# Feed-forward activations turned by transposing transfers of 16 bit halves instead of by TensorE

## The chip, the cores and the metric

The kernel runs on one core of a Trainium2 chip. The metric is the device time of one execution in microseconds (us), the median of several runs. Engines are named as the profile names them: PE is TensorE (matrix products and transposes) and PEld its weight loader, DVE is VectorE, ACT is ScalarE, POOL is GpSimd and SP the engine that issues most transfers. A "q" behind an engine's name (ACTq, SPq) stands for its issuing of transfers.

## The reference

One decoder layer for 256 tokens and a model width of 2048. The part that matters here is the feed-forward at its end, in float32:

```
h = x + concatenate([gla_out, nsa_out]) @ w_out
m = rms_norm(h, ffn_norm_g)
return h + (silu(m @ w_gate) * (m @ w_up)) @ w_down        # w_gate, w_up: 2048 x 5632, w_down: 5632 x 2048
```

The attention parts ahead of it are not touched by the change.

## The kernel before

The feed-forward runs over 11 blocks of 512 hidden columns (NFB = 11, FB = 512). For each block f, `gate_up(f)` forms the gate and up products in PE's banks, eight pairs of row tiles at a time, most of them with seven products instead of eight (the banks q = 1, 5, 6, 7 hold sums that are combined on DVE afterwards). Its last steps give two tiles `g` of 128 tokens by 512 hidden values, kept in `hidden[f]`. `down(f)` multiplies them with `w_down`, and needs them turned: hidden values on the partitions. The program runs gate_up(0), gate_up(1), down(0), gate_up(2), down(1) and so on; the last block has a `down_last` of its own.

All products use float32 operands split into two rounded parts, hi and lo: ACT copies a tile into hi with rounding, DVE subtracts to get lo (`in_parts`, lines 654 to 657). The same is done with every weight tile that arrives: `fraw` is the raw tile, `ftwo` its parts, and `fsum` and some tiles `g` are sums of weight rows.

The turn is `turn_act(fb, qs)`: for each of the two tiles, four 128 x 128 transposes on PE (line 213, with the identity `ident`) into a bank, then hi and lo of that bank into `acts[fb]`, which `down` reads. It is a generator in the queue `urgent`; while the main generator `gate_up(fb + 1)` emits products, `drive` calls `side` now and then, which lets the first waiting side task take its next step. A number that a task yields puts it to sleep for that many calls. For block 0 the turn is queued near the end of gate_up(1), for blocks 1 to 9 at the start of the next gate_up, and for block 10 ahead of down(9). Within `gate_up`, a pair that is not among the "sevens" drains `urgent` first, because its products and the turns share bank 8.

Within `down`, each of four stretches n of 512 output columns is started from `h_sb[n]`, which ACT copies into two banks (`seed`, line 1281), and its results are copied back out of the banks by ACT (line 1293). Those banks are then used by the next `gate_up`.

What a side task emits is not executed at once: a scheduler lays the instructions of each engine out in one fixed order before the program runs, and each engine works through its own in that order. An instruction that has to wait holds up everything behind it on its engine, including the issue of transfers. Tiles named `f` come from a pool of six (`g2` in this stage), tiles `g` from one of 24.

Of the kernel before, what the change touches and what calls it, by code (L numbers as in the profile page):

```python
# [7 lines left out]

F32 = mybir.dt.float32
F32R = mybir.dt.float32r  # L10
BF16 = mybir.dt.bfloat16
AF = mybir.ActivationFunctionType
ALU = mybir.AluOpType
# [2 lines left out]
P = 128  # L16
S = 256
# [20 lines left out]
def kernel(  # L38
# [4 lines left out]
    nc = tc.nc  # L43
    act, mm = nc.scalar.activation, nc.tensor.matmul
# [22 lines left out]
    g4, g2, g1, small = slot(gp, "g4", 24, LINE), slot(s2p, "g2", 13), slot(s1p, "g1", 7), slot(s1p, "sm", 12)  # L67
# [8 lines left out]

    def f32(t):
        return t.bitcast(F32)


    urgent, later, background = [], [], []
# [41 lines left out]

    def weight(tag, nk, w, bufs, dt=F32R):
        n_tiles[0] += 1
# [227 lines left out]
    def first_chunk(q):  # L353
        nonlocal first_rest
        hi, lo = g4([4, S], F32R), g4([4, S], F32R)
        n_h.append(hi)
# [285 lines left out]
    def gla_turn(h, y):  # L642
        yield 26
        if h % 2 == 0:
            m_h[h // 2], m_l[h // 2] = g4([4, S], F32R), g4([4, S], F32R)
        p = bank()
# [7 lines left out]
    def in_parts(hi, lo, ps, after=None):  # L654
        with behind(after):
            act(hi, ps, AF.Copy)  # L656
        last["d"] = TT(lo, ps, f32(hi), ALU.subtract)  # L657
# [505 lines left out]
    def gate_up(fb):  # L1163
        def product(q, a, w, k):

            if q not in banks:
                banks[q] = bank()
            for x, m in ((a[0], w[k][0]), (a[0], w[k][1]), (a[1], w[k][0])):
                mm(banks[q], x, m, start=todo[q] == total[q], stop=todo[q] == 1)  # L1169
                todo[q] -= 1  # L1170

        def tokens(k, t):
            assert k in turned
            return tuple(x[k // 4][:, k % 4, t * P:(t + 1) * P] for x in (hT_h, hT_l))

        order, sevens = (ORDER0, ORDER1, ORDER)[0 if fb == 0 else 1 if fb < ALL7 else 2], FIRST7.get(fb, PAIRS7)
        last7 = max(sevens, key=order.index)
        todo = dict.fromkeys((1, 5, 6, 7), 3 * len(sevens))
        todo.update(dict.fromkeys((2, 3, 4), 3 * len(sevens) + 6 * (8 - len(sevens))))
        todo[8] = 6 * (8 - len(sevens))  # L1180
        total = dict(todo)
        if fb > 1:
            urgent.append(turn_act(fb - 1, (8, 8)))
        for at, pair in enumerate(order):
            if fb > 1 and pair not in sevens:
                drain(urgent)
            if fb == 0 and at == len(OLD):
                ffn_pools()
            a, b = 2 * pair, 2 * pair + 1
            ready = row_sums.get((fb, pair))  # L1190
            if at < 7:
                fetch_sums(fb, order[at + 1])
            r = load4([(w_gate[0], a, 2, fb * FB), (w_up[0], a, 1 if ready else 2, fb * FB)])
            if ready:
                s1, s2 = fetched.pop((fb, pair))
            if pair in sevens:
                w = parts_of(r[:, 0:3])
                if not ready:
                    s1, s2 = g4([2, 512]), fw["sum"]([2, 512])
                    TT(s1, r[:, 1:3], r[:, 3:4].to_broadcast([P, 2, 512]), ALU.add)  # L1200
                    TT(s2[:, 0], s1[:, 1], r[:, 1], ALU.add)
                    TT(s2[:, 1], s2[:, 0], r[:, 0], ALU.add)  # L1202
                f = [tuple(forms[pair][:, i, j] for i in range(2)) for j in range(4)]
                raw = {1: (tokens(b, 0), 1), 2: (tokens(a, 0), 0), 3: (f[3], 2)}
                of_sums = {5: (f[0], 0), 7: (f[2], 1), 6: (f[1], 2), 4: (tokens(a, 1), 3)}

                for q in (6, 1, 5, 7, 2, 3, 4) if at == 7 else (1, 2, 3, 5, 7, 6, 4):
                    if q in of_sums and len(of_sums) == 4:
                        ws = parts_of2(s1, s2)
                        if ready:  # L1210
                            ws = [ws[k] for k in (1, 0, 3, 2)]
                    if q in raw:
                        x, k = raw[q]
                        product(q, x, w, k)
                    else:
                        x, k = of_sums.pop(q)
                        product(q, x, ws, k)
                    yield 2
            else:
                w = parts_of(r)  # L1220
                for q, t, m in ((2, 0, 0), (3, 0, 1), (4, 1, 0), (8, 1, 1)):
                    for j in range(2):
                        product(q, tokens(a + j, t), w, 2 * m + j)
                        yield 2
            if pair == last7:
                q1, u, q5u, q7u, q57u = (g2([512]) for _ in range(5))
                act(q1, banks[1], AF.Copy)
                TT(u, banks[6], q1, ALU.add)
                TT(q5u, banks[5], u, ALU.subtract)
                TT(q7u, banks[7], u, ALU.add)  # L1230
                TT(q57u, banks[5], q7u, ALU.subtract)
                if fb == 1:
                    urgent.append(turn_act(0, (1, 5)))
                if fb:
                    seed(0, DOWN[min(fb - 1, 1)])
        if fb == 0:
            drain(urgent)
            rms(rf, ssh)
            TT(rf, rf, hback, ALU.mult)
        gs = hidden[fb] = []  # L1240
        for t, (g, gq, u_, uq) in enumerate(((q1, 2, q5u, 3), (q7u, 4, q57u, 8))):
            TT(g, banks[gq], g, ALU.add)
            act(g, g, AF.Silu, scale=rf[:, t:t + 1])
            if total[uq]:
                TT(u_, banks[uq], u_, ALU.add)
            STT(g, u_, rf[:, t:t + 1], g, ALU.mult, ALU.mult)
            gs.append(g)

    hidden, acts = {}, {}

    def turn_act(fb, qs):
        for _ in range(2):
            yield
        gs = hidden.pop(fb)
        hi, lo = acts[fb] = g4([4, S], F32R), g4([4, S], F32R)
        for t in range(NT):
            ts = slice(t * P, (t + 1) * P)
            p = banks[qs[t]]
            for j in range(4):
                transpose(p[:, j * P:(j + 1) * P], gs[t][:, j * P:(j + 1) * P])  # L1260
                if j % 2:
                    yield
            pv = p.rearrange("p (j s) -> p j s", j=4)
            in_parts(hi[:, :, ts], lo[:, :, ts], pv)
        if fb == NFB - 1:
            for pair in range(2):
                yield
                yield
                v, ks = g2([2, S]), slice(2 * pair, 2 * pair + 2)
                TT(v, f32(hi[:, ks]), f32(lo[:, ks]), ALU.add)  # L1270
                pair_forms(8 + pair, v)
# [164 lines left out]
```

## Time and profile before

| | us |
|---|---|
| median of three runs | 1102.14 (1101.81 to 1103.24) |
| the profiled execution, its own time | 1101.13 |
| its span, first to last instruction | 1099.1 |
| PE busy | 1094.3 |
| DVE busy | 996.3 |
| ACT busy | 744.5 |
| POOL busy | 81.1 |

The granted clock of PE is 1.000 throughout. The profile lists groups of instructions by line, engine and operation (busy time, mean duration in ns, idle time before them and who ended it), a table of busy time by stretch, each engine's instructions in order of time with the idle time before each in brackets, and the transfers with the time from issue to landing.

### The profile page before, as it was taken

To read this page: it belongs to the slowest core of one execution; us is meant where nothing else is said; L and a number is where in the kernel's file an instruction comes from. 1 tells how busy PE (TensorE), PEld (TensorE's weight loads), DVE (VectorE), ACT (ScalarE), POOL (GpSimd) and SP (SyncE) were. 2 spreads that over 40 slices of the span, in tenths; PEclk is the share of its full clock that TensorE was granted. 3 is DMA by queue.
4 is the path that set the end of the run, shared out by engine and by line. 5 is a ranking of instruction groups with operands and counts; after the bars stand their busy time and mean duration, and the time that the engine had idled before them with its cause. 6 is when DMAs were issued, how large, how long until landed. Compare 5 with 4: busy or idle time off the path is not lost.

```text
span 1099.1 us, 14686 instructions
## 1 busy us (share of the span) xinstructions
PE 1094.3 (100%) x5294; PEld 900.8 (82%) x5294; DVE 996.3 (91%) x1289; ACT 744.5 (68%) x1014; POOL 81.1 (7%) x150
## 2 busy tenths in 40 slices
PE   9999999999999999999999999999999999999998
PEld 8888888987777887888888888888888888888887
DVE  6578879987799988997999999999999999999998
ACT  7645567555675587667585867768585877768685
POOL 4110001033100100000000000000000000000000
PEclk9999999999999999999999999999999999999999
DMA  7999978468886946785566657576665768677663
GB/s 271 340 338 369 394 259 284 167 243 290 307 280 246 331 159 244 234 317 190 182 230 209 211 197 253 184 248 209 213 230 202 251 214 294 208 259 232 235 231 115
DMA packets 128818, 271.15 MB, mean 247 GB/s; under 512 B 7093, under 2 KB 9177, under 8 KB 128746
## 3 DMA queue, kind: packets, MB, share of 16 engines
q1 hardware_dynamic: 115466, 223.61, 59.2%
q0 software_dynamic: 12672, 46.14, 11.3%
q8 instruction: 41, 0.67, 0.2%
q10 hardware_dynamic: 608, 0.47, 0.1%
q14 instruction: 31, 0.25, 0.1%
HBM read 247.12 MB, written 23.07 MB: 246 GB/s over the span
## 4 chain that ended last, share of the span: by engine, by line
PE 89%; DVE 3%; DMA 3%; issue 2%; ACT 2%; POOL 0%; SPq 0%; DVEq 0%; ACTq 0%; POOLq 0%
PE bank L289 41%; PE bank L1169 39%; PE bank L213 3%; DMA g<-in_w_up_dram 2%; PE bank L1310 2%; DVE lo L145 2%; PE bank L967 1%; PE bank L893 1%; DMA raw<-in_w_out_dram 1%; DVE g L1101 1%; ACT hi L144 1%; PE bank L598 0%; PE bank L800 0%; PE bank L203 0%; ACT g L559 0%
## 5 line engine op out<-in xcount | busy, mean ns | idle before, releaser
L1169 PE MATMUL bank<-ftwo,g 128*128 128x512 f32 x1842 | 430.7, 393 | 0.2 <-ACT ftwo L656 0.2
L1169 PEld LDWEIGHTS bank<-ftwo,g 128*128 128x128 f32 x1842 | 341.2, 188 | 77.0 <-DVE ftwo L657 4.0
L289 PE MATMUL bank<-hi,g 128*128 128x512 f32 (+1 forms) x1088 | 322.7, 377 | 0.0
L657 DVE TENSOR_TENSOR ftwo<-fraw,ftwo 128x1536 fp32r<-128x1536 f32 (+1 forms) x130 | 256.8, 1976 | 7.7 <-ACT ftwo L656 6.6
L656 ACT ACTIVATE ftwo<-fraw 128x1536 fp32r<-128x1536 f32 (+1 forms) x130 | 216.0, 1663 | 28.9 <-DMA fraw<-in_w_up_dram 19.1
L289 PE MATMUL bank<-ftwo,g 128*128 128x512 f32 x960 | 220.7, 390 | 0.0
L289 PEld LDWEIGHTS bank<-hi,g 128*128 128x128 f32 x1088 | 191.9, 189 | 30.3 <-issue 1.0
L289 PEld LDWEIGHTS bank<-ftwo,g 128*128 128x128 f32 x960 | 179.7, 188 | 38.3 <-ACT bank L1281 0.3
L144 ACT ACTIVATE hi<-raw 128x1024 fp32r<-128x1024 f32 (+3 forms) x124 | 130.4, 1058 | 94.7 <-PE bank L289 67.1
L289 PE MATMUL bank<-lo,g 128*128 128x512 f32 (+3 forms) x544 | 193.3, 376 | 0.4 <-DVE lo L145 0.3
L145 DVE TENSOR_TENSOR lo<-raw,hi 128x1024 fp32r<-128x1024 f32 (+3 forms) x124 | 149.8, 1217 | 29.6 <-ACT hi L144 29.3
L656 ACT ACTIVATE ftwo<-g 128x1024 fp32r<-128x1024 f32 x76 | 80.4, 1057 | 73.2 <-DVE g L1200 49.9
L289 PEld LDWEIGHTS bank<-lo,g 128*128 128x128 f32 x544 | 98.2, 189 | 15.2 <-DVE lo L145 1.0
L657 DVE TENSOR_TENSOR ftwo<-g,ftwo 128x1024 fp32r<-128x1024 f32 x76 | 92.8, 1221 | 10.3 <-ACT ftwo L656 10.3
L657 DVE TENSOR_TENSOR ftwo<-fsum,ftwo 128x1024 fp32r<-128x1024 f32 x76 | 92.7, 1220 | 1.0 <-ACT ftwo L656 1.0
L656 ACT ACTIVATE ftwo<-fsum 128x1024 fp32r<-128x1024 f32 x76 | 79.6, 1048 | 5.5 <-DVE fsum L1202 3.9
L1293 ACT COPY g<-bank 128x512 f32<-128x512 f32 x80 | 45.9, 588 | 38.6 <-PE bank L289 36.9
L1200 DVE TENSOR_TENSOR g<-fraw 128x1024 f32<-128x1024 f32 x54 | 65.3, 1220 | 0.3 <-DMA fraw<-in_w_up_dram 0.3
L1281 ACT COPY bank<-g 128x512 f32<-128x512 f32 x80 | 45.3, 594 | 14.7 <-DVE f L1230 8.4
L1158 POOL DMA_DIRECT2D g<-sums x20 | 10.6, 531 | 502.1 <-DVE ftwo L657 473.6
L656 ACT ACTIVATE g<-bank 128x512 fp32r<-128x512 f32 x46 | 26.9, 597 | 29.7 <-PE bank L213 21.2
L213 PE MATMUL bank<-ident,g 128*128 128x128 f32 (+3 forms) x230 | 42.9, 277 | 0.1
(249 smaller groups left out, 913.2 us busy)
## 6 DMA issues: line engine op xcount, KB each, us to landing
fraw<-in_w_gate_dram SPq DMA_DIRECT2D x86, 512.0 KB, 4.0
fraw<-in_w_down_dram SPq DMA_DIRECT2D x42, 1024.0 KB, 5.0
raw<-in_w_in_dram SPq DMA_DIRECT2D x36, 1024.0 KB, 7.8
fraw<-in_w_up_dram SPq DMA_DIRECT2D x66, 512.0 KB, 4.8
sums<-g POOLq DMA_DIRECT2D x40, 512.0 KB, 6.5
raw<-in_w_out_dram SPq DMA_DIRECT2D x16, 1024.0 KB, 7.3
g<-in_w_gate_dram SPq DMA_DIRECT2D x20, 512.0 KB, 7.5
g<-in_w_up_dram SPq DMA_DIRECT2D x20, 512.0 KB, 7.8
```

What stands on the lines that cost most here:

```text
L144: act(h[:, i:i + n], r[:, k + i:k + i + n], AF.Copy)
L145: last["d"] = TT(o[:, i:i + n], r[:, k + i:k + i + n], f32(h[:, i:i + n]), ALU.subtract)
L213: return nc.tensor.transpose(o, i, ident[:n, :n])
L289: last["mm"] = mm(bk[t], a[:, k, t * P:(t + 1) * P], ws[k][m][:, off:off + w], start=(first_ and k == 0 and i == 0), stop=(end and k == 3 ...
L656: act(hi, ps, AF.Copy)
L657: last["d"] = TT(lo, ps, f32(hi), ALU.subtract)
L893: mm(sv, a[:, j], b, start=(i == 0), stop=False, skip_group_check=True)
L1169: mm(banks[q], x, m, start=todo[q] == total[q], stop=todo[q] == 1)
L1200: TT(s1, r[:, 1:3], r[:, 3:4].to_broadcast([P, 2, 512]), ALU.add)
L1281: last["seed", n] = nc.scalar.copy(banks[qs[n][t]], h_sb[n][:, t, :])
L1293: nc.scalar.copy(h_sb[n][:, t, :], bs[t])
L1310: mm(bk, u, m, start=(first and i == 0), stop=(end and i == 2), skip_group_check=onto)
```

## The change

`turn_far` takes the place of `turn_act` for blocks 0 to 9. It treats each float32 value as two 16 bit halves. For each tile, ACT copies the halves apart (all upper, all lower) into a tile `u`, and issues a transposing transfer from `u` back into the tile `g`, in 16 bit elements. Six calls of `side` later, ACT copies the halves together again into `u`, and hi and lo are made from `u`. For block 0 the turn is queued at the start of gate_up(1) instead of its end. Block 10 keeps `turn_act`.

```diff
+    def u16(t):
+        return t.bitcast(U16)
+
+    def halves(t):
+        return u16(t).rearrange("p (h c) -> p h c", h=2)
...
-        if fb > 1:
-            urgent.append(turn_act(fb - 1, (8, 8)))
+        if fb:
+            urgent.append(turn_far(fb - 1))
...
-                if fb == 1:
-                    urgent.append(turn_act(0, (1, 5)))
...
+    def turn_far(fb):
+        for _ in range(2):
+            yield
+        gs = hidden.pop(fb)
+        hi, lo = acts[fb] = g4([4, S], F32R), g4([4, S], F32R)
+        us = []
+        for g in gs:
+            u = g2([512])
+            us.append(u)
+            act(halves(u), u16(g).rearrange("p (c h) -> p h c", h=2), AF.Copy)
+            nc.scalar.dma_start_transpose(u16(g).rearrange("p (b s) -> p b s", s=P), u16(u))
+            yield
+        yield 6
+        for t, g in enumerate(gs):
+            act(u16(us[t]).rearrange("p (c h) -> p h c", h=2), halves(g), AF.Copy)
+            yield
+            in_parts(hi[:, :, t * P:(t + 1) * P], lo[:, :, t * P:(t + 1) * P], us[t].rearrange("p (j s) -> p j s", j=4))
```

In the changed file line numbers are higher by 7 up to the new function and by 23 behind it: L656 and L657 become L663 and L664, L1293 becomes L1316. The copies that separate the halves are L1265, the transfers L1266, the copies that join them L1270.

How the order moves is shown where down(4) and gate_up(6) meet, with the turn of block 5 in between. First ACT before: `ftwo_6930` and `ftwo_6947` are the parts of gate_up(6)'s pair 0 and of its sums, `ftwo_6973` and `ftwo_6996` those of pair 1, `ftwo_7018` those of pair 2; the copies of L1293 empty down(4)'s banks for n = 2 (g_636) and n = 3 (g_683), and `g_1116` is hi of the turned block.

```order
L656 ACTIVATE ftwo_6947<-g_1113_6933 128x1024
L1293 COPY g_636_3524<-bank_4334 128x512
L1293 COPY g_636_3524<-bank_4353 128x512
L656 ACTIVATE ftwo_6973<-fraw_6970 128x1536
L656 ACTIVATE ftwo_6947<-fsum_6934 128x1024
L1293 COPY g_683_3739<-bank_4370 128x512
L1293 COPY g_683_3739<-bank_4448 128x512
L656 ACTIVATE ftwo_6996<-g_1120_6976 128x1024
L656 ACTIVATE ftwo_6996<-fsum_6977 128x1024
L656 ACTIVATE ftwo_7018<-fraw_7015 128x1536
L656 ACTIVATE g_1116_6958<-bank_4382 128x4x128 x2
```

The two copies into hi come at the end, behind the copies out of the banks. ACT in the changed kernel, from the same instruction (`f_1108` and `f_1111` are the block's tiles, `f_1128` and `f_1129` the tiles u; bank_4448 is bank 1 of gate_up):

```order
L663 ACTIVATE ftwo_6947<-g_1123_6933 128x1024
L1265 ACTIVATE f_1128_6960<-f_1108_6777 128x1024
L1265 ACTIVATE f_1129_6966<-f_1111_6780 128x1024
L1266 DMA_TRANSPOSE f_1108_6777<-f_1128_6960 128x8x128
L1316 COPY g_636_3524<-bank_4334 128x512
L1316 COPY g_636_3524<-bank_4353 128x512
L663 ACTIVATE ftwo_6947<-fsum_6934 128x1024
L1266 DMA_TRANSPOSE f_1111_6780<-f_1129_6966 128x8x128
L663 ACTIVATE ftwo_6975<-fraw_6972 128x1536
L1270 ACTIVATE f_1128_6960<-f_1108_6777 128x2x512
L1316 COPY g_683_3739<-bank_4370 128x512
L1316 COPY g_683_3739<-bank_4448 128x512
```

Two copies, two issues and the first joining copy, which waits for its transfer, now stand ahead of the copies out of the banks for n = 3. The rest of the turn follows behind them:

```order
L663 ACTIVATE ftwo_7012<-fraw_7009 128x1536
L663 ACTIVATE g_1126_6958<-f_1128_6960 128x4x128
L1270 ACTIVATE f_1129_6966<-f_1111_6780 128x2x512
L663 ACTIVATE ftwo_7030<-g_1137_7015 128x1024
L663 ACTIVATE g_1126_6958<-f_1129_6966 128x4x128
L663 ACTIVATE ftwo_7030<-fsum_7016 128x1024
```

On PE, what stands behind those copies is the start of gate_up(6). In the changed kernel:

```order
L296 MATMUL bank_4448<-ftwo_6898,g_1072_6506 128x512 x2
L296 MATMUL bank_4448<-ftwo_6898,g_1073_6507 128x512
L1176 MATMUL bank_4334<-ftwo_6930,g_722_3967 128x512 x2
L1176 MATMUL bank_4334<-ftwo_6930,g_723_3968 128x512
L1176 MATMUL bank_4353<-ftwo_6930,g_742_4046 128x512
L1176 MATMUL bank_4448<-ftwo_6930,g_722_3967 128x512 x2
L1176 MATMUL bank_4448<-ftwo_6930,g_723_3968 128x512
```

The first two rows are the last products of down(4), into the bank that L1316 copies out last; the fifth product of gate_up(6) writes that bank again. This stands the same before and after; only the four pieces of the transposes (L213) are gone from the rows further on.

More of the change, by code (lines that the diff above doesn't have):

```diff
@@ L10 @@
 F32R = mybir.dt.float32r
+U16 = mybir.dt.uint16
 BF16 = mybir.dt.bfloat16
```

## The prediction

> **What bounds the kernel now.** First the chain of work that ended last (shares of the span by engine), then a table of busy time by block.
>
> ```profile
> PE 89%; DVE 3%; DMA 3%; issue 2%; ACT 2%; POOL 0%; SPq 0%; DVEq 0%; ACTq 0%; POOLq 0%
> ```
>
> The table cuts the feed-forward stage where the products of down() begin. A stretch holds down(f) and then gate_up(f + 2): the one from 744.20 holds down(4) and gate_up(6), with the turn of block 5 in it.
>
> ```profile
> core 0: us, PE busy (x) PEld busy (x) DVE busy (x) ACT busy (x) POOL busy (x), PEclk, DMA share, GB/s
> 496.50:558.45 61.95, 61.95 (x278) 50.66 (x276) 55.89 (x52) 41.49 (x45) 1.06 (x2) 1.00 0.54 187
> 558.45:620.30 61.85, 61.85 (x276) 50.63 (x275) 60.84 (x57) 44.26 (x47) 1.05 (x2) 1.00 0.64 217
> ...
> 806.20:868.10 61.90, 61.90 (x276) 50.63 (x275) 60.84 (x58) 44.25 (x47) 2.11 (x4) 1.00 0.66 227
> ...
> 990.80:1051.90 61.10, 61.10 (x273) 49.96 (x272) 59.67 (x56) 46.16 (x50) 2.10 (x4) 1.00 0.71 236
> ```
>
> PE is never idle at full clock, so PE time that disappears is time gained, until something else stops it. DVE is the first candidate: 60.84 of 61.85 us in the five stretches from 558 to 868 (the first and last are shown). ACT has 17 us of room per block, but it works in a fixed order, so what counts is where the room lies.
>
> What the turns cost is read from the starts of PE's groups, not from their durations, which overlap.
>
> ```profile
> 744.21 22.03 PE L289 MATMUL bank<-ftwo,g 128*128 128x512 f32 x96
> 766.08 3.69 PE L1169 MATMUL bank<-ftwo,g 128*128 128x512 f32 x15
> 769.60 0.38 PE L213 MATMUL bank<-ident,f 128*128 128x128 f32 x2
> 769.74 0.95 PE L1169 MATMUL bank<-ftwo,g 128*128 128x512 f32 x3
> 770.53 0.38 PE L213 MATMUL bank<-ident,f 128*128 128x128 f32 x2
> 770.66 2.32 PE L1169 MATMUL bank<-ftwo,g 128*128 128x512 f32 x9
> 772.82 0.60 PE L213 MATMUL bank<-ident,f 128*128 128x128 f32 x4
> 773.18 33.19 PE L1169 MATMUL bank<-ftwo,g 128*128 128x512 f32 x144
> ```
>
> 96 products of down() take 766.08 - 744.21 = 21.87 us, 0.228 us each. From 766.08 to 773.18 there are 27 products and 8 transposes: 7.10 - 27 x 0.228 = 0.95 us for a block's eight transposes.
>
> Now ACT in the same place, with its idle time in brackets. The L1293 copies carry down()'s results out of the banks (n = 1, 2, 3 in turn).
>
> ```profile
> 757.61 1.07 ACT L656 ACTIVATE ftwo<-g 128x1024 fp32r<-128x1024 f32 x1
> 760.21 1.27 ACT L1293 COPY g<-bank 128x512 f32<-128x512 f32 x2 [1.53 <-PE bank L289]
> 761.38 1.49 ACT L656 ACTIVATE ftwo<-fraw 128x1536 fp32r<-128x1536 f32 x1
> 762.77 1.05 ACT L656 ACTIVATE ftwo<-fsum 128x1024 fp32r<-128x1024 f32 x1
> 765.65 1.27 ACT L1293 COPY g<-bank 128x512 f32<-128x512 f32 x2 [1.84 <-PE bank L289]
> 766.82 1.06 ACT L656 ACTIVATE ftwo<-g 128x1024 fp32r<-128x1024 f32 x1
> 767.77 1.05 ACT L656 ACTIVATE ftwo<-fsum 128x1024 fp32r<-128x1024 f32 x1
> ```
>
> And PE's weight loader just behind the second pair of copies:
>
> ```profile
> 766.97 2.14 PEld L1169 LDWEIGHTS bank<-ftwo,g 128*128 128x128 f32 x10 [0.25 <-ACT g L1293]
> ```
>
> This row decides the case. The copies from 765.65 empty bank 1, which gate_up(6) needs for its fifth product. They end at 766.92, and the loader, having waited 0.25 us, starts at 766.97. So there is no slack: whatever makes ACT late at these copies makes PE idle by as much. ACT has only the two waits of 1.53 and 1.84, 3.37 us, ahead of them.
>
> **The change, part by part.**
>
> *Gone from PE:* ten blocks' transposes (block 10 keeps its own), 10 x 0.95 = 9.5 us on the path. Also gone are the waits of ACT on them; those lie behind the copies and free nothing ahead of them.
>
> *Added on ACT, per block:* two copies that separate the halves (L1265), two transposing transfers (L1266), two copies that join them (L1270). Each copy handles 1024 elements a partition; the nearest row has 4-byte elements:
>
> ```profile
> L656 ACT ACTIVATE ftwo<-g 128x1024 fp32r<-128x1024 f32 x76 | 80.4, 1057 | 73.2 <-DVE g L1200 49.9 <-PE bank L1169 21.2 <-issue 1.6
> ```
>
> One starts 0.95 us behind the one before it (766.82 to 767.77), so I take 0.96. It could be cheaper with half the bytes or dearer with a stride of two; I give it 0.2 us either way, under 1 us a block.
>
> In the changed order two separating copies and one joining copy come ahead of the decisive copies: 2.88 us, which leaves 3.37 - 2.88 = 0.49 us for two transfer issues. With d the time for which an issue holds ACT, PE then waits s = 2d - 0.49 per block. The other joining copy, and both copies into hi, come after that point, where ACT has room.
>
> *The issue, d.* No row shows a transposing transfer. The nearest one is a plain transfer issued by ACT:
>
> ```profile
> 1079.23 0.37 ACTq L1322 DMA_DIRECT2D out_dram<-g  x1
> 1079.64 1.06 ACT L656 ACTIVATE ftwo<-fsum 128x1024 fp32r<-128x1024 f32 x1 [0.17 <-ACT g L1321]
> ...
> 1080.99 0.34 ACTq L1322 DMA_DIRECT2D out_dram<-g  x1
> ```
>
> ACT goes on 0.41 us after the issue began: the low end. The new one names its output as 8 x 128 columns; if the queue handles each block of columns as a command of its own, eight at 0.34 us make 2.7 us: the high end. I take the middle, 1.5 us: the work is plainly more than one plain command, and nothing shows that each block costs a full one. An end below 0.41 is excluded, since a transposing transfer carries everything a plain one does.
>
> [...]
>
> *The landing, L.* A joining copy waits for its transfer, and everything behind it in ACT's order waits too, the decisive copies first. Plain transfers land after (KB each, median us from issue; the two of 256 KB are as large as the new ones):
>
> ```profile
> fraw<-in_w_down_dram SPq DMA_DIRECT2D x42, 1024.0 KB, 5.0
> ...
> fraw<-in_w_up_dram SPq DMA_DIRECT2D x20, 256.0 KB, 4.9
> ...
> out_dram<-g SPq DMA_DIRECT2D x4, 256.0 KB, 2.9
> out_dram<-g ACTq DMA_DIRECT2D x3, 128.0 KB, 2.4
> ```
>
> I take 3.9 us, ends 2.9 and 4.9. Behind the first issue ACT has two copies, an `fsum` copy, the second issue and a `fraw` copy to do: 1.2 + 0.95 + d + 1.4 = 3.5 us + d, so L is covered even at d = 0.41. In gate_up(3) the two issues stand together with only the `fraw` copy behind them; there the cover is 1.4 + d, 2.9 us at d = 1.5, and 1.0 us shows.
>
> *The other blocks.* gate_up(6), (7) and (8) have the order above: 2.51 us each at d = 1.5. In (3) and (5) a copy into hi (0.5 us) also stands ahead of the second copy: 3.0 each, (3) with the 1.0 of landing. In (4) the second joining copy too: 4.0. In (9) and (10) no joining copy stands ahead, and the room was
>
> ```profile
> 945.42 0.59 ACT L1293 COPY g<-bank 128x512 f32<-128x512 f32 x1 [1.54 <-PE bank L289]
> ...
> 950.86 1.27 ACT L1293 COPY g<-bank 128x512 f32<-128x512 f32 x2 [2.03 <-PE bank L289]
> ```
>
> 1.54 + 2.03 - 1.92 = 1.65, so 3.0 - 1.65 = 1.35 each. In (2), where DVE has 6 us to spare, ACT's waits were
>
> ```profile
> 507.06 1.27 ACT L1293 COPY g<-bank 128x512 f32<-128x512 f32 x2 [2.29 <-PE bank L289]
> ...
> 510.18 1.06 ACT L656 ACTIVATE ftwo<-fsum 128x1024 fp32r<-128x1024 f32 x1 [0.90 <-DVE fsum L1202]
> 512.50 1.32 ACT L1293 COPY g<-bank 128x512 f32<-128x512 f32 x2 [1.26 <-PE bank L289]
> ...
> 517.94 1.27 ACT L1293 COPY g<-bank 128x512 f32<-128x512 f32 x2 [2.73 <-PE bank L289]
> ```
>
> 7.18 us against 4.3 us of copies and 3.0 of issues: 0.1. In gate_up(1) no down() runs beside it: 0.
>
> *DVE.* Its two subtractions per block read SBUF instead of a bank at the same price, so its work stays:
>
> ```profile
> L657 DVE TENSOR_TENSOR g<-bank,g 128x512 fp32r<-128x512 f32 x40 | 27.2, 685 | 2.9 <-ACT g L656 2.9
> ...
> L657 DVE TENSOR_TENSOR g<-f,g 128x512 fp32r<-128x512 f32 x4 | 2.7, 684 | 0.0
> ```
>
> It takes its operands from ACT and already stood 0.77 us for one here:
>
> ```profile
> 767.91 1.23 DVE L657 TENSOR_TENSOR ftwo<-g,ftwo 128x1024 fp32r<-128x1024 f32 x1 [0.77 <-ACT ftwo L656]
> ```
>
> In the changed order the `fraw` copy of pair 1 ends at 764.1 + 2d instead of 762.8, and DVE would want it at about 765.8; at d = 1.5 it starves by some 1.8 us in all, so a block costs it 60.87 + 1.8 + 0.3 of other idle time = 62.9 us. That is under PE's 61.93 - 0.95 + 2.51 = 63.5, so PE's wait sets the block. Without any lateness of ACT, DVE's 60.87 + 0.3 = 61.2 us would cap the gain at 0.76 us a block.
>
> *Transfers.* 0.5 MB more per block is little beside a DMA share of 0.64; no SP instruction moves past another. Some weight loads also wait for a transpose's semaphore, but only some eight transfers later.
>
> *Sum at d = 1.5:* PE's waits 0 + 0.1 + 4.0 + 4.0 + 3.0 + 3 x 2.51 + 2 x 1.35 = 21.3 us, less 9.5: +11.8 us. The profiled execution took 1101.13 us (span 1099.1 and 2.0 around it), 1.0 below the median of 1102.14; the sum gives 1112.9 there, 1113.9 against the median.
>
> **The rivals.**
>
> *The issue is a plain one* (ends faster). At d = 0.41 and L = 2.9 the waits are 1.9 in (3), 1.8 in (4), 0.8 in (5), 0.3 each in (6) to (8), none elsewhere: 5.5 us against 9.5, 1098 us. For it: the plain issues last 0.34 and 0.37 us, and nothing in the trace shows a dearer one on ACT. Against: it needs the cheapest end of both unknowns; with L = 4.9 the waits come to 12.7 us and it ends at 1105. It decides below 2d = 1.5, where the waits equal 9.5. [...]
>
> *No change:* d of 0.7 to 0.9, the waits eat what PE saves: 1100 to 1104. Nothing favours just this price.
>
> *Each block of columns costs a command or more, or the landing is long.* At d = 2.7 the waits are 2.5 + 5.4 + 6.4 + 5.4 + 3 x 4.9 + 2 x 3.75 = 41.9: 1134.5 us. If eight pieces landed one after the other at 2.4 us or more each, joining copies would hold ACT over 10 us a block, and 1200 us would be passed. The eight-fold output speaks for it; against a serial landing stands that the queues move 1 MB in 5 us.
>
> **How the numbers follow.** A change of less than 0.2% (2.2 us) can hardly be told from none. d between 0.9 and 2.7: 0.63, with the forecast of 1114 us. Longer issues or landings, above 1135: 0.10. No change: 0.12. Plain issue: 0.15. So slower 0.73, same 0.12, faster 0.15. The range runs from the plain issue's 1097 to 1135.
>
> **What would show it.** In the changed profile: 8 transposes of `f` instead of 88; issues of the new kind on ACT's queue with ACT resuming about 1.5 us later; ACT's wait for PE ahead of the second pair of copies gone; PE's loader waiting about 2.5 us for the copies in (6) to (8), 3 to 4 in (3) to (5); DVE idle 1 to 2 us more per block. The prediction is wrong if ACT resumes after 0.4 us, if the copies of 2-byte elements run at another pace, or if PE still waits 0.25 us there.

## The result, and the profile after

The changed kernel takes 1116.97 us in the median of four runs (1113.77 to 1118.56), against 1102.69 for the kernel before in the same comparison: a ratio of 1.0126, 95% interval 1.0101 to 1.0150. That is slower by 1.3%. The forecast of 1114 us was near the time, but the time was not lost in the places it named. The profiled execution took 1118.56 us, span 1116.8, mean granted clock 0.994.

The first part of the page, busy time by engine:

```profile
PE 1094.3 (98%) x5214; PEld 896.8 (80%) x5214; DVE 996.0 (89%) x1289; ACT 786.1 (70%) x1054; POOL 81.3 (7%) x150
```

80 transposes have gone, and yet PE is as long busy as before (1094.3). So some of its work took longer than before; 12.3 us of it ran at half clock, as shown below. ACT has 41.6 us more.

ACT's new groups (busy time, mean ns | idle time ahead and what ended it):

```profile
L1270 ACT ACTIVATE f<-f 128x1024 uint16<-128x1024 uint16 x20 | 27.3, 1366 | 13.7 <-DMA f<-f 13.7
L1265 ACT ACTIVATE f<-f 128x1024 uint16<-128x1024 uint16 x20 | 20.3, 1054 | 0.5 <-DVE f L1251 0.5
```

The view of the line that issues the new transfers: the issue's duration (min/median/max in ns), who waited for them, and the time to landing:

```profile
L1266 ACTq DMA_TRANSPOSE f<-f x20: 1247/1248/3749, 459.6 to 1027.4; - x20
...
  ACT f L1270: 13.7, 7
...
DMA to landing us min/median/max: 4.2/6.0/11.0
```

The separating copies cost what was assumed, the joining ones (L1270) 0.3 us more. An issue lasts 1.25 us in the median and 3.75 at the most. The landing takes 6.0 us, above the upper end of 4.9 that I had taken from plain transfers. For seven of the 20 landings ACT stood waiting, 13.7 us in all.

The table by stretch, cut where down(f) begins as in the prediction. The first row holds down(0) and gate_up(2), the last down(8) and gate_up(10). Columns: length, busy time of PE, PEld, DVE, ACT, POOL, PE's granted clock, transfers.

```profile
504.91:569.45 64.54, 62.27 (x268) 49.65 (x267) 59.66 (x53) 46.86 (x49) 1.06 (x2) 1.00 0.69 213
569.45:632.42 62.97, 61.08 (x269) 49.91 (x267) 60.27 (x59) 49.56 (x53) 1.06 (x2) 1.00 0.67 219
632.42:700.45 68.03, 63.86 (x269) 52.01 (x268) 60.74 (x55) 48.63 (x52) 1.06 (x2) 0.95 0.66 204
700.45:761.35 60.90, 60.88 (x269) 50.00 (x268) 60.37 (x57) 48.54 (x52) 1.06 (x2) 1.00 0.73 229
761.35:822.18 60.83, 60.83 (x269) 49.91 (x267) 60.19 (x57) 48.42 (x52) 1.06 (x2) 1.00 0.72 229
822.18:884.25 62.07, 61.51 (x269) 49.75 (x268) 60.20 (x57) 48.18 (x52) 2.12 (x4) 1.00 0.78 236
...
1007.47:1069.38 61.91, 60.92 (x265) 49.08 (x264) 59.73 (x56) 49.73 (x54) 2.11 (x4) 1.00 0.75 243
```

Before, the first six of these stretches took 61.9 to 62.0 us and the last three 61.2 to 61.4. The ones of gate_up(5) and (6) are shorter by 1.05 and 1.17 us: the promised gain, and no loss. Those of (7) to (10) are longer by 0.1 to 0.75. The loss lies in three places: gate_up(1), whose end (the start of down(0)) moved from 496.49 to 504.91, +8.4 us; gate_up(2), +2.6; gate_up(4), +6.1. With +1.1 in (3) the sum over all ten is 17.5 us. These are the profiled executions, 17.4 us apart; the medians are 14.3 us apart.

**gate_up(1), where I had put down nothing.** Block 0's turn is now its first side task. ACT and DVE, then POOL, then PE, in the order in which one holds up the next (brackets: idle time and what ended it):

```profile
465.14 1.36 ACT L1270 ACTIVATE f<-f 128x1024 uint16<-128x1024 uint16 x1 [2.17 <-DMA f<-f]
...
471.50 1.37 ACT L1270 ACTIVATE f<-f 128x1024 uint16<-128x1024 uint16 x1 [2.73 <-DMA f<-f]
...
474.63 1.04 ACT L663 ACTIVATE ftwo<-fsum 128x1024 fp32r<-128x1024 f32 x1
...
468.29 2.29 DVE L664 TENSOR_TENSOR ftwo<-fraw,ftwo 128x2048 fp32r<-128x2048 f32 x1 [3.57 <-ACT ftwo L663]
...
474.23 1.76 DVE L664 TENSOR_TENSOR ftwo<-fraw,ftwo 128x1536 fp32r<-128x1536 f32 x1 [3.05 <-ACT ftwo L663]
...
477.12 1.22 DVE L664 TENSOR_TENSOR ftwo<-fsum,ftwo 128x1024 fp32r<-128x1024 f32 x1
...
478.63 0.53 POOL L1165 DMA_DIRECT2D fsum<-sums  x1 [13.08 <-DVE f L1044]
479.15 1.05 POOL L1165 DMA_DIRECT2D g<-sums  x2
...
484.20 1.06 ACT L663 ACTIVATE ftwo<-g 128x1024 fp32r<-128x1024 f32 x1 [2.86 <-DMA g<-sums]
...
485.31 19.77 PE L1176 MATMUL bank<-ftwo,g 128*128 128x512 f32 x72 [5.36 <-ACT ftwo L663]
```

ACT waits for two landings, DVE starves behind ACT, and both come late to the sums in `fsum`: ACT's copy at 474.63, then DVE's subtraction from 477.12 to 478.34 (before, it ended at 472.68). POOL has a fetch in its queue that writes `fsum` again and has to wait for DVE, and behind it two fetches of row sums that the profile shows waiting for nothing else. The profile names a combination of forms (L1044) as what ended POOL's wait. The times speak for the subtraction instead: POOL's other fetches in this stretch that wait for DVE start 0.29 to 0.30 us after DVE has read a tile of the name that they write, and this one starts 0.29 us after 478.34. Before, the same two fetches stood ahead of that one and left together with a third:

```profile
466.47 1.56 POOL L1158 DMA_DIRECT2D g<-sums  x3
```

They are 12.7 us late, and PE, which works on those sums, is idle for 5.36 us.

**gate_up(2).** Here the loader waits seven times, for 0.2 to 1.5 us and 4.8 us in all, six times for DVE's parts of the weights. DVE is busy for 59.7 us in this stretch, where it was for 55.9 before. Why its work has moved into this stretch was not found. That block 0 comes late is not enough: in experiment 5, where it does, the same stretch takes 60.9 us.

**gate_up(4).** Here the two issues stand together, and ACT is late at the copies out of the banks:

```profile
645.06 1.25 ACTq L1266 DMA_TRANSPOSE f<-f  x1
...
646.35 3.75 ACTq L1266 DMA_TRANSPOSE f<-f  x1
650.14 0.59 ACT L1316 COPY g<-bank 128x512 f32<-128x512 f32 x1 [3.40 <-issue]
...
656.82 1.34 ACT L1270 ACTIVATE f<-f 128x1024 uint16<-128x1024 uint16 x1 [2.01 <-DMA f<-f]
...
659.01 0.57 ACT L1316 COPY g<-bank 128x512 f32<-128x512 f32 x1
...
659.64 10.58 PE L1176 MATMUL bank<-ftwo,g 128*128 128x512 f32 x33 [4.17 <-ACT g L1316]
```

The second issue lasts three times as long as the first and holds ACT for 3.40 us; the joining copy waits 2.01 us for its landing; the copies of n = 3 end at 659.6, and PE waits for them, 4.17 us.

**The clock.** The same table in stretches of about 5 us, behind PE's idle times in gate_up(1), (4) and (3). The column ahead of the last two is the granted clock:

```profile
485.00:490.00 5.00, 4.65 (x10) 3.26 (x11) 4.56 (x4) 5.00 (x6) 0.53 (x1) 0.50 0.36 110
490.00:495.00 5.00, 5.00 (x20) 4.01 (x20) 5.00 (x5) 3.72 (x3) 0.00 (x0) 0.84 0.83 276
...
660.00:665.00 5.00, 5.00 (x13) 3.84 (x13) 4.53 (x5) 3.49 (x4) 0.00 (x0) 0.50 0.08 28
665.00:670.00 5.00, 5.00 (x22) 4.13 (x21) 3.13 (x5) 3.57 (x3) 0.00 (x0) 0.93 0.59 197
...
590.00:595.00 5.00, 3.11 (x15) 2.25 (x14) 3.30 (x4) 4.82 (x6) 0.00 (x0) 1.00 0.46 87
595.00:600.00 5.00, 5.00 (x24) 4.12 (x23) 4.52 (x5) 5.00 (x6) 0.00 (x0) 1.00 0.57 207
```

Behind the idle times of 5.36 and 4.17 us PE goes on at half clock (13 products in 5 us instead of 24). Cut finer, the clock is 0.50 from 484.8 to 491.6 and from 658.9 to 665.7, 6.8 us each, and 1.00 on both sides, so 0.84 and 0.93 are averages; PE works for 6.3 and 6.0 us of these times. Behind an idle time of 1.89 us in gate_up(3) the clock does not fall. A stretch at 0.50 and one at 0.84 lose 2.3 + 0.8 = 3.1 us; at 0.50 and 0.93, 2.9 us. So both large losses add up: gate_up(1) is 5.4 of idle time + 0.8 of a second wait behind it + 3.1 of clock - 0.95 = 8.3 (8.4 measured); gate_up(4) is 4.2 + 2.9 - 0.95 = 6.1 (6.1). Idle times of 1.94 and 2.08 us in experiments 6 and 10 were followed by some 3.4 us at half clock, an estimate from the numbers given there. The prediction had not counted the clock.

### The profile page after: what moved, and what is told of

The parts are those of the page before. It is cut to its first block, busy times and chain, and to the rows that moved or that the text cites. A ratio compares the mean times of both kernels' runs of the same rounds, so it can differ in the third digit from the quotient of the medians.

```text
span 1116.8 us, 14518 instructions
## 1 busy us (share of the span) xinstructions
PE 1094.3 (98%) x5214; PEld 896.8 (80%) x5214; DVE 996.0 (89%) x1289; ACT 786.1 (70%) x1054; POOL 81.3 (7%) x150
## 5 line engine op out<-in xcount | busy, mean ns | idle before, releaser
L1176 PE MATMUL bank<-ftwo,g 128*128 128x512 f32 x1842 | 432.9, 395 | 17.4 <-ACT ftwo L663 7.7
L1176 PEld LDWEIGHTS bank<-ftwo,g 128*128 128x128 f32 x1842 | 346.9, 190 | 101.7 <-ACT ftwo L663 10.9
L664 DVE TENSOR_TENSOR ftwo<-fraw,ftwo 128x1536 fp32r<-128x1536 f32 (+1 forms) x130 | 255.9, 1976 | 14.0 <-ACT ftwo L663 13.8
L663 ACT ACTIVATE ftwo<-fraw 128x1536 fp32r<-128x1536 f32 (+1 forms) x130 | 214.5, 1660 | 20.4 <-PE bank L1176 13.2
L296 PEld LDWEIGHTS bank<-ftwo,g 128*128 128x128 f32 x960 | 179.5, 188 | 38.5 <-ACT bank L1304 0.7
L663 ACT ACTIVATE ftwo<-g 128x1024 fp32r<-128x1024 f32 x76 | 80.3, 1057 | 73.8 <-DVE g L1207 61.6
L664 DVE TENSOR_TENSOR ftwo<-g,ftwo 128x1024 fp32r<-128x1024 f32 x76 | 92.8, 1220 | 10.3 <-ACT ftwo L663 10.0
L664 DVE TENSOR_TENSOR ftwo<-fsum,ftwo 128x1024 fp32r<-128x1024 f32 x76 | 92.5, 1220 | 3.4 <-ACT ftwo L663 3.4
L663 ACT ACTIVATE ftwo<-fsum 128x1024 fp32r<-128x1024 f32 x76 | 79.8, 1051 | 16.7 <-DVE fsum L1209 15.6
L1316 ACT COPY g<-bank 128x512 f32<-128x512 f32 x80 | 45.2, 583 | 13.7 <-PE bank L296 8.0
L1112 POOL DMA_DIRECT2D sums<-g x40 | 21.9, 548 | 263.2 <-DVE g L1108 208.5
```

The source lines that it names most:

```text
L296: last["mm"] = mm(bk[t], a[:, k, t * P:(t + 1) * P], ws[k][m][:, off:off + w], start=(first_ and k == 0 and i == 0), stop=(end and k == 3 ...
L1112: nc.gpsimd.dma_start(part, a)
L1316: nc.scalar.copy(h_sb[n][:, t, :], bs[t])
```

## The experiments

All are compared with the kernel before, measured beside them on the same chip: 1101.2 to 1101.4 us there.

**1. Block 0 back on TensorE, at its old place.**

```diff
-        if fb:
+        if fb > 1:
             urgent.append(turn_far(fb - 1))
...
                 TT(q57u, banks[5], q7u, ALU.subtract)
+                if fb == 1:
+                    urgent.append(turn_act(0, (1, 5)))
```

> Block 0 is turned by TensorE at its old place (banks 1 and 5, after the fifth pair of gate_up(1)); blocks 1 to 9 keep the transfers. The stretch up to down(0) lost 8.4 us in the changed kernel. Theory (the loss there comes from the place: the turn is now the first task of gate_up(1), ACT waits for its landings, DVE's forms and the row sums come late behind it): the stretch falls back by 8 to 8.5 us, and the time is 1117 - 8.4 = 1108.6 us, 1107 to 1110. Rival (the transfers cost what they cost wherever they are, by contention or a lower clock, and the blocks after would give the same time away): 1114 to 1117 us.

Measured: 1101.36 us, ratio 1.0009 (0.9997 to 1.0022). No loss is left, nor any gain. The stretch up to down(0) fell back by 8.6 us, as expected, but the whole by 15.6, so the expected 1108.6 us was missed. The rest came from gate_up(2) and (4), which in the profiled executions went from 64.5 and 68.0 to 61.6 and 60.9 us. The cause is in the program's order: with other work in gate_up(1), the scheduler also laid out the next blocks otherwise. In gate_up(4) the issues now lie 2.2 us apart, and ACT waits for no issue, only 0.58 us for PE:

```profile
635.28 1.25 ACTq L1268 DMA_TRANSPOSE f<-f  x1
636.78 1.27 ACT L1318 COPY g<-bank 128x512 f32<-128x512 f32 x2 [0.58 <-PE bank L296]
637.47 1.25 ACTq L1268 DMA_TRANSPOSE f<-f  x1
```

The second joining copy, too, now stands behind the copies for n = 3 (at 647.02; it stood ahead of them at 656.82). So the same work costs 6 us or gains 1 us in one block, by where the second issue and that copy stand. What block 0 costs by itself is not measured by this run; experiment 5 does that.

**2. The turn held behind the copies out of the banks, the issues apart.** Block 0 as in 1. The separating and joining copies are tied behind the latest copy of weights in program order, and the turn sleeps longer between its steps.

```diff
-        for _ in range(2):
-            yield
+        yield 6
...
+            with behind(last["pa"]):
                 act(halves(u), u16(g).rearrange("p (c h) -> p h c", h=2), AF.Copy)
             nc.scalar.dma_start_transpose(u16(g).rearrange("p (b s) -> p b s", s=P), u16(u))
-            yield
+            yield 7
         yield 6
...
-            if fb > 1 and pair not in sevens:
-                drain(urgent)
```

> Block 0 on TensorE as above; for blocks 1 to 9 the separating copies are held until after the last copy out of down()'s banks, the two transfers are issued some five instructions apart, and the joining copies come some five instructions after the second issue. The work is the same. Theory (what costs time is ACT's lateness at the copies out of the banks, from issues, separating copies and waits for landings ahead of them): PE keeps the 0.95 us per block for 9 blocks, 1102.7 - 8.6 = 1094 us, 1093 to 1098; no wait of PE's loader on the copies out of the banks is over 0.5 us. Rival 1 (the transfers disturb the weight loads or DVE is the next bound): 1100 to 1105 us, with waits of PE on DVE or DMA. Rival 2 (the added ACT work is too much wherever it lies): 1106 us or more.

Measured: 1096.30 us, ratio 0.9957 (0.9942 to 0.9972): faster than both kernels, with the same copies and transfers in blocks 1 to 9. What PE's loader waited for (total, times, longest):

```profile
PEld bank L1176 <- DVE ftwo L664: 4.5, 16, 0.6
...
PEld bank L1176 <- ACT g L1317: 2.3, 8, 0.5
```

And the transfers, in the view of their line:

```profile
L1266 ACTq DMA_TRANSPOSE f<-f x18: 1247/1248/1332, 522.4 to 1017.5; - x18
...
DMA to landing us min/median/max: 3.1/4.6/7.8
```

At the copies out of the banks eight waits of 0.3 are left, as before the change. No issue is held and no landing waited for, and the granted clock is 1.000. ACT's lateness at certain places was the cost, not the amount of its work: its busy time is as in the changed kernel (787.7 us).

**3. As 2, but the two issues right behind each other in blocks 3 to 9** (the sleeps are 6, 4 and 9 calls instead of 6, 7 and 6).

> As the run before (behind the copies out of the banks), but the two transfers of blocks 3 to 9 are issued right behind each other, and the joining copies follow six or seven instructions later. In the changed kernel a second issue right behind the first held ACT for 3.75 us against 1.25. Theory (a held issue costs only where ACT has a deadline close behind it): the second issues take 3.7 us again, and the time is within 3 us of the run with the issues apart, 1094 to 1098 us. Rival (2.5 us of ACT are lost in each of 7 blocks and PE waits for the parts of the weights): 1100 to 1112 us.

Measured: 1103.99 us, ratio 1.0020 (1.0007 to 1.0032). That is 7.7 us over experiment 2: the rival, and my theory failed. From 497 to 1000 us ACT stands behind issues five times, 9.6 us in all and at most 2.0 at a time, which it never does in experiment 2. Here it is 1.76:

```profile
709.09 2.64 ACTq L1266 DMA_TRANSPOSE f<-f  x2
711.78 1.06 ACT L663 ACTIVATE ftwo<-g 128x1024 fp32r<-128x1024 f32 x1 [1.76 <-issue]
```

The first row of the loader's waits:

```profile
PEld bank L1176 <- DVE ftwo L664: 10.2, 22, 1.2
```

DVE gets its operands later, and the loader waits 10.2 us for DVE's parts instead of 4.5. In this order the middle of a gate_up has no room for it either.

**4. The copies alone.** TensorE turns as before; the four copies of blocks 1 to 9 are added near their place in the changed kernel, without transfers, into tiles that nobody reads.

```diff
-            nc.scalar.dma_start_transpose(u16(g).rearrange("p (b s) -> p b s", s=P), u16(u))
...
+        yield from turn_act(fb, (8, 8))
```

> Blocks 0 to 9 are turned by TensorE as in the kernel before; for blocks 1 to 9 ACT also makes the two separating and the two joining copies near their place in the changed kernel, with no transfer between them (the joined tiles are not used). In the order all four stand ahead of the last copies out of down()'s banks: 2 x 0.96 + 2 x 1.25 = 4.4 us against 3.4 us of waits that ACT had there. Theory (no slack at these copies): PE waits about 1.0 us per block, 1102.7 + 9 = 1112 us, 1107 to 1114. Rival (the copies fit into ACT's idle time, only issues and landings cost): 1102 to 1104 us.

Measured: 1112.20 us, ratio 1.0103 (1.0087 to 1.0118): the theory's 1112. The blocks became 1.1 us longer (63.0 to 63.1 us between the starts of down(1) to down(6)). All four copies stand ahead of the decisive copies there, and the loader shows the missing slack:

```profile
646.27 12.79 PEld L1176 LDWEIGHTS bank<-ftwo,g 128*128 128x128 f32 x57 [0.82 <-ACT g L1315]
```

It waited 0.25 us there before. These 0.57 us are half of the 1.1; the rest shows in other waits of the loader, the longest one 0.55 us for ACT's parts of the weights late in the block. So the time agrees with the slack of 3.4 us that the prediction read from two of ACT's waits, but the run does not measure this slack by itself.

**5. Block 0 by itself.** Experiment 2, with block 0 as in the changed kernel (unheld, first in gate_up(1)); the orders of ACT and POOL there are the changed kernel's.

> Blocks 1 to 9 apart, as in the run of 1096.3 us; block 0 by transfers at the start of gate_up(1), and in that stretch the orders of ACT and POOL are those of the changed kernel. Theory (the 8.4 us of that stretch come from block 0's turn standing ahead of DVE's forms and so of POOL's fetches of the row sums, and stay there): the stretch up to down(0) is 8 to 9 us longer than in the run of 1096.3 us, the loader waits 5 to 6 us in one piece behind POOL's late fetch, and the time is 1096.3 + 8.4 = 1104.7 us, 1103 to 1107. Rival (block 0 alone costs the 15 us by which the changed kernel stood above the run with only block 0 undone, because the lower clock behind a long idle time of TensorE and ACT's lateness go on into the next blocks): 1109 to 1113 us.

Measured: 1104.23 us, ratio 1.0021 (1.0008 to 1.0034), 7.9 us over experiment 2; expected 8.4. The stretch up to down(0) is 6.7 us longer, less than the 8 to 9 expected. The same wait stands at its end:

```profile
484.23 0.50 PEld L1176 LDWEIGHTS bank<-ftwo,g 128*128 128x128 f32 x2 [5.61 <-ACT ftwo L663]
```

And the table by stretch shows the same fall of the clock, to 0.53 on average in these 5 us:

```profile
485.00:490.00 5.00, 4.96 (x13) 3.63 (x12) 4.85 (x5) 5.00 (x6) 0.53 (x1) 0.53 0.47 135
```

**6. All ten blocks apart**, block 0's turn queued at the fourth pair of gate_up(1), behind DVE's forms (`if fb == 1 and at == 3: urgent.append(turn_far(0))`).

> All ten blocks by transfers, all of them apart and behind: block 0's turn starts at the fourth pair of gate_up(1), behind DVE's forms. Theory: block 0 gains its 0.95 us too, 1096.3 - 0.95 = 1095.3 us, 1094 to 1097, and the fetches of the row sums are not later than in the kernel before. Rival (ACT's added work in gate_up(1), where it had fewer idle times, or landings that are waited for ahead of the copies into the banks, cost more than TensorE saves): 1097 to 1102 us.

Measured: 1102.56 us, ratio 1.0005 (0.9990 to 1.0020), 12 runs from 1098.4 to 1105.4. The theory missed. POOL's fetches are in time again, but now the two joining copies stand ahead of the copies that fill down(0)'s banks, and PE starts down(0) and stops:

```profile
495.82 1.07 PE L296 MATMUL bank<-ftwo,g 128*128 128x512 f32 x4
498.82 23.10 PE L296 MATMUL bank<-ftwo,g 128*128 128x512 f32 x92 [1.94 <-ACT bank L1305]
```

The stretches around and behind it:

```profile
490.00:500.00 10.00, 8.05 (x34) 5.96 (x33) 9.34 (x13) 10.00 (x14) 0.00 (x0) 0.97 0.60 222
500.00:505.00 5.00, 5.00 (x18) 3.96 (x18) 5.00 (x4) 2.17 (x2) 0.00 (x0) 0.71 0.21 50
```

The gain of 1 us at 495.82 (496.83 in experiment 2) is lost and more: down(1) begins 3.0 us later than there (561.11 against 558.12). Behind an idle time of 1.94 us the clock fell here: it is 0.97 and 0.71 on average in these stretches and 1.00 in the next, which by estimate makes 3.4 us at half clock, from about 499.5 to 502.9. The fastest of the runs is the one with a mean clock of 1.000, the others have 0.996 to 0.999.

**7. The transfers alone.** TensorE turns as before; in blocks 1 to 9 two transposing transfers a block are issued near the changed kernel's place, without copies, into tiles that nobody reads.

> Blocks 0 to 9 are turned by TensorE as before; in blocks 1 to 9 ACT also issues two transposing transfers near their place in the changed kernel (on the unseparated tiles, into tiles that are not used), without any copy. Theory: two issues of 1.25 us, partly beside the instruction before, against 3.4 us of waits ahead of the copies out of the banks: no loss where the second is not held, 1101 to 1103 us; if each block's second issue is held as in three blocks of the changed kernel (3.75 us), 1.25 + 3.75 - 3.4 = 1.6 us a block, 1115 us; I expect few to be held: 1101 to 1106. Rival (the transfers slow the weights' loads or copies by what they move, 0.5 MB a block): 1107 us or more, with waits on DMA.

Measured: 1106.08 us, ratio 1.0045 (1.0030 to 1.0061), just above the 1101 to 1106 that I had expected. Most issues lie apart, and the two of a block show what one costs ACT:

```profile
696.21 1.25 ACTq L1263 DMA_TRANSPOSE f<-f  x1
696.57 0.61 ACT L1310 COPY g<-bank 128x512 f32<-128x512 f32 x1
...
700.49 1.25 ACTq L1263 DMA_TRANSPOSE f<-f  x1
702.11 0.59 ACT L1310 COPY g<-bank 128x512 f32<-128x512 f32 x1 [1.06 <-issue]
```

The first issue holds nothing: a copy runs beside it. The second holds ACT for 1.06 us. The loader's waits at the copies out of the banks stay at 0.25 us each. Each of the first six stretches is 0.5 to 0.7 us longer than before, by small waits on parts of weights and of the activations; the two behind them lose 0.2 us at most, and the last, down(8) and gate_up(10), loses 3.0, with waits of up to 1.7 us for DVE's parts. Which of them the transfers cause, and how, stays open.

**8. Experiment 2 with the transfers issued by SP** (`nc.sync` for `nc.scalar`).

> As the run of 1096.3 us (block 0 on TensorE, blocks 1 to 9 apart), but the transfers are issued by SP between its loads of weights. Theory (issues of 1.25 us cost ACT nothing where it has idle time; SP has to wait for the separating copy, with loads queued behind it, but loads run ahead of their use): 1096 to 1098 us, the same within 2 us. Rival 1 (issues on ACT still cost PE something): 1092 to 1095 us. Rival 2 (SP held by the separating copy makes loads late): 1099 us or more, with waits on DMA of the weights.

Measured: 1096.50 us, ratio 0.9955 (0.9940 to 0.9971). No difference from experiment 2: apart issues cost ACT nothing that matters, and SP's loads did not come late in a way that shows (ACT waited 5.9 us for weights there, 5.1 in experiment 2).

**9 to 11. What limits the apart version.** It keeps 4.9 of the 8.6 us that PE saves in nine blocks.

> The bound of the gain: in blocks 1 to 9 the turn is left out altogether (the parts of the activations are taken from the untransposed tiles at the late place), so TensorE has no transposes there, ACT no separating or joining copies and no issues, and nothing is transferred; block 0 on TensorE. If TensorE alone set the time: 1101.3 - 9 x 0.95 = 1092.7 us. Theory (of the 8.6 us the apart version keeps only 5, since DVE, busy 60.4 us of a stretch of 61.3, is the next bound): 1095 to 1097 us, no more than 1.5 us under the apart version. Rival (the missing 3.6 us are ACT's 6 us of added work a block): 1091.5 to 1094 us.

> The apart version, with four additions of bank and partial sum on DVE (0.69 us each, two pairs at a block's end) left out in blocks 1 to 10: 2.8 us less of DVE per block, ACT and the transfers unchanged. Theory (DVE is what limits the apart version): TensorE's waits on DVE and on the parts that come late behind it go, 1092 to 1094.5 us. Rival (ACT's added work or the transfers limit it): within 1 us of the apart version, 1095.5 to 1097.

> The apart version without its transfers: the separating and the joining copies stay where they are (they put the halves apart and back together), nothing is issued or moved, the parts are taken from untransposed tiles. Theory (well placed, the transfers cost nothing): the same as the apart version within 1 us, 1095.5 to 1097.3 us. Rival (the transfers' issues or their 0.5 MB a block cost part of the missing 3.6 us): 1092.5 to 1095 us.

Measured: 1095.22 us without any turn in blocks 1 to 9 (ratio 0.9944, 0.9928 to 0.9961); 1102.75 with less of DVE's work (1.0009, 0.9996 to 1.0021); 1095.58 without the transfers (0.9949, 0.9934 to 0.9963). Even with no turn at all only 6.0 of the 8.6 us are gained, so ACT's copies and the transfers account for about 1 us of what is missing. The 6.0 us are 0.67 a block, near the 0.76 that the prediction had put as the cap by DVE. But that DVE's amount of work limits the rest, as I thought, is not shown: experiment 10 came out above both of its ranges. With 2.4 us less of it a stretch (58.1 busy us for 60.5) the stretches from down(0) to down(5) have the length that they have in experiment 2 (306.5 us against 307.0). The run is slower because the order changed again: from down(6) on, ACT fills down()'s banks too late, there behind a copy of weights that waits for its transfer. PE's idle time is 0.99 us there, 1.72 and 2.08 us in the next two blocks. Behind the 1.72 us 63 products take 14.46 us (936.03 to 950.49), 0.230 each; behind the 2.08 us the same 63 take 16.05 (998.77 to 1014.82), and the mean clock of this execution is 0.998. Against 0.228 us a product that is 1.69 us more, by estimate 3.4 us at half clock.

```profile
870.83 1.92 ACT L663 ACTIVATE ftwo<-fraw 128x2048 fp32r<-128x2048 f32 x1 [1.10 <-DMA fraw<-in_w_down_dram]
...
873.89 13.02 PEld L296 LDWEIGHTS bank<-ftwo,g 128*128 128x128 f32 x58 [1.42 <-ACT bank L1306]
```

What holds the last 2.5 us back stays open.

**12. Idle times made on purpose**, to test the clock without transfers: in the kernel before, 4, 6 and 7 extra ACT copies ahead of the last copies out of the banks in down(2), (4) and (6).

> The kernel before with extra copies on ACT (128x1024, 0.96 us each, into a tile that is not used) held ahead of the last copies out of down()'s banks in three blocks: 4, 6 and 7 of them, in down(2), down(4) and down(6); where the order lets a part of the weights (1.4 us) go ahead too, it counts with them. No transfers. With 3.4 us of waits ahead of these copies, TensorE should be idle for about 0.5 to 1.9, 2.4 and 4.7 us in one piece, 7.6 to 9 us in all. Theory (an idle time of over some 2.3 us makes the granted clock fall to a half for about five microseconds when work comes back, as behind the 5.4 and 4.2 us of the changed kernel, not behind its 2.3): no fall behind the first, 0 to 1.5 us more behind the second, about 3 us more behind the third; mean clock 0.995 to 0.997, 1101.3 + 8.3 + 3 = 1112.6 us, 1110.5 to 1115.5. Rival (the lower clock there came with the transfers): clock 1.000 and 1108.9 to 1110.3 us.

Measured: 1108.12 us, ratio 1.0059 (1.0042 to 1.0077), clock 1.000. Neither case was tested, since no long idle time came about. The scheduler moved products of PE, too, and the loader's waits stayed short (9 waits for parts of weights, 1.3 us at most):

```profile
PEld bank L1169 <- ACT ftwo L656: 7.1, 9, 1.3
```

That the clock falls by idle time alone is thus not shown apart from the transfers; it rests on idle times of different length in kernels that have them.

## Why the prediction was right in sum, and where it failed

**Right:** the sign, and the mechanism for a part of the loss. PE's gain of 0.95 us a block is there (gate_up(5) and (6), -1.05 and -1.17). The copies out of down()'s banks are a decisive place in (3), (4) and (8), and experiments 2 and 4 agree with the little room read there. But PE was idle at these copies for 6.9 us in all (1.89, 4.17 and 0.82), where the sum had 21.3 us of waits. A dearer issue than a plain one is there: 1.25 us, I had taken 1.5 between 0.41 and 2.7.

**Wrong: s = 2d - 0.49 for every block.** The step took the issue's duration for time that ACT loses. An issue that stands by itself costs ACT between nothing and 1.4 us (1.06 in experiment 7; 1.41 behind the changed kernel's issue at 900.09); two together cost 1.8 to 3.6 in the changed kernel and experiment 3, and nothing at one place in experiment 7 (the second issue, at 504.80, lasts 2.23 us, and ACT's next wait ends with PE's products). So the loader waited 0.2 us at the copies in (6) and (7), for which I had 2.51 each, and the stretch of (5) became shorter, where I had a wait of 3.0. In (3) it waited 2.3 (4.0 forecast), in (8) 1.24 (2.51), in (4) 4.6 (4.0). In (3) and (4) the two issues stood together. In (9) and (10) it waited 1.07 and 1.42 (1.35 forecast), but for parts of the weights and not at the copies.

**Wrong: gate_up(1) at 0 and gate_up(2) at 0.1.** I asked only whether down()'s copies run beside, and there is no down() in gate_up(1). The turn's new place, with joining copies that wait for landings ahead of ACT's next copies for DVE, and POOL's queue were in the order to be seen: two fetches had moved behind one that waits for DVE. That was 8.4 us, or 7.9 by experiment 5. In (2) I saw no single large wait before and none after, but seven small ones of 0.2 to 1.5 us.

**Mis-sized: the landing L**, 3.9 with ends of 2.9 and 4.9; measured 6.0 in the median, up to 11.0, and 4.6 where the transfers are apart (experiment 2). Seven of the 20 landings were waited for, two of them in gate_up(1). The joining copy was put at 0.96 us; start to start it takes 1.23 (465.14 to 466.37).

**Missing: the clock.** No term of the sum held it, and it made 6 us of the 17.5 in the profiled execution.

**Wrong as a rule: DVE idle 1 to 2 us more per block.** It is idle for 0.5 us in (5) and 0.6 in (6), where it was for 1.1 before, for 4.9 in (2), where it was for 6.1, and for 7.3 in (4). Only (3), (7), (8) and (10) come near what I named, with 0.8 to 1.7 us more.

The sum of +11.8 came near the measured +14.3 (+17.5 in the profiled execution) because six blocks that I had priced too dear, (3) and (5) to (9), stood against (1), (2), (4) and (10), which I had too cheap. It was right by compensation, not block by block. The rival of the plain issue was nearer to the truth than the forecast in blocks (5) to (7), and over (5) to (10) together: it gives -4.0 us there, the forecast +7.5, and -0.7 were measured.

## What to carry to other kernels

Work that moves from the limiting engine to one that works in a fixed order is paid by what stands behind it there: look for the next deadline (a copy out of a bank, a queue with a waiting fetch at its head), and place the new work behind it. The same copies and transfers in nine blocks leave the time as it was at one place (experiment 1) and gain 0.4% at another (experiment 2); in the changed kernel, with block 0 at its early place, they cost 1.3%. After an edit, read the whole order again, of blocks that the edit doesn't touch too, and add to a long idle time of TensorE what its clock takes afterwards, here about 3 us behind 4.2 and 5.4 us.

## What the runs showed of the hardware

A transposing transfer of 128 x 1024 two-byte elements held ACT's queue for 1.25 us in the median (1.29 in experiment 3), at times for longer when it stood by itself (1.95 in the changed kernel at 900.09, up to 2.07 in experiments 5 and 10), and one right behind another for about 1.3 (experiment 3, two in 2.64) to 3.75 (changed kernel). Why the second issue is held was not found. It landed after 4.2 to 11.0 us in the changed kernel, 6.0 in the median, after 3.1 to 7.8 in experiment 2 and after 3.0 to 13.3 in experiment 6; plain transfers of the same 256 KB took 2.9 to 4.9 in the median in the kernel before. An ACT copy of 128 x 1024 two-byte elements took 1.37 us where its results are written at a stride of two (L1270, 1366 ns), and 1.05 where only the source is strided (L1265, 1054 ns).

TensorE's granted clock was at half for 6.8 us in the changed kernel, around the end of idle times of 4.17 and 5.36 us, and by estimate for 3.4 us at idle times of 1.94 and 2.08 us (experiments 6 and 10). Behind 1.89 us (gate_up(3) of the changed kernel) it stayed at 1.00, and behind 1.72 us (experiment 10) the products kept to 0.230 us each. Whether the length of the idle time alone decides this is not shown.
